# Order of quarter products, their additions and the first down pages in a transformer block

## The chip, the cores and the metric

The kernel runs on one core of a Trainium2 chip. The metric is the device time of one execution in microseconds. Engines: PE (TensorE, matmuls), DVE (VectorE), ACT (ScalarE), POOL (GpSimd), SP (SyncE, which here only issues DMAs). Each engine works through its own queue of instructions in order and waits on semaphores for the others.

## The reference, cut

One layer on x of 1024 x 1024 (float32), D_FF = 2816:

```
h = rmsnorm(x, norm1_g); proj = h @ w_in
mixed = concat(forgetting_attention(q, k, v, log_f), multiscale_pool(u))
x = x + mixed @ w_out
h2 = rmsnorm(x, norm2_g)
gate = h2 @ w_gate
up = h2 @ w_up
x = x + (silu(gate) * up) @ w_down
return rmsnorm(x, final_g)
```

The change lies in the products with w_gate, w_up and w_down.

## The kernel before, in words

**Numbers.** A float32 matrix is kept as two fp32r halves: `split` (L119 to L121) lets ACT copy the hi half (L120) and DVE subtract it for the lo half (L121). A product of two such matrices is three matmuls (`mm3`, L161 to L163: hi·hi, hi·lo, lo·hi), added up in a PSUM bank.

**Gate/up stage.** The 2816 columns are 22 tiles of 128, taken as 11 pairs j = 0 to 10. Each pair is computed by a scheme of seven block products P1 to P7 (in the manner of Strassen and Winograd) instead of eight. Their left operands are blocks of the normed activations (b11, b21, t1 to t4, b22), made once; their right operands are sums of the pair's weight blocks (`gu_sums`, L1070 to L1073, on POOL), split into "pages". From pair 1 on the order is P1, P2, P6, P7, P5, P3a, P4, P3b. A page is made two products ahead (`next_page`).

**The quartered third product.** For j ≥ 1, P3 is itself computed by seven quarter products Q1 to Q7 of 256 columns (`fine_product`), in three banks: A takes Q1, Q6, Q5, Q3 in turn, B takes Q7, Q4, and C takes Q2. After each quarter DVE adds the bank's state into a copy in SBUF (the "sU4" snapshot, L1249), and the next quarter in that bank waits for this add. The page of P3 is made in two parts (P3a, P3b) after subtractions on DVE (`fine_page`, L1214). The quarter sums of the block b22 are made once, in pair 1 (`fine_steps`, up to three steps after each product: DVE's L1189 and L1196 in before, then a split); Q4's operand overwrites b22h/b22l.

**What leaves a pair.** `corner` makes the features h11, h22 and h21: DVE adds bank and snapshot into q (L1154; one buffer), ACT applies silu (L1155), DVE forms h (L1156), POOL multiplies (L1157) and so frees q. h12 is made of the snapshot after P3b (L1272, L1273). `feature_sum` makes f1 to f4 of these (L1162). `spill` stores the features to DRAM (L1254), as a DMA on ACT's queue, behind which ACT waits for the feature; the last pair's last ones go on POOL's queue.

**Down stage.** 28 steps (4 groups of pairs, 7 products each): w_down is loaded (`down_raw`, L1356), summed on POOL for the first group (`down_sum`, L1364), the features are loaded back (`down_load`, L1375), both are split into pages (`down_page`, tiles d0_0 to d0_3 and so on: features hi and lo, weights hi and lo), multiplied into banks d, and added to the residual x2f (L1512). The final norm follows.

**What sets the order.** A scheduler with a simulated timeline orders each engine's instructions; `tc.issue_after(ins)` pins what is issued inside it behind an instruction of the same engine. `mark["mm"]` is the last matmul written so far, `mark["hi"]` ACT's last hi half.

Of the kernel before, what the change touches and what calls it, by code (L numbers as in the profile page):

```python
# [15 lines left out]
P = 128  # L16
# [29 lines left out]
def tile_kernel(  # L46
# [1099 lines left out]
    def corner(j, name, key, src, to):  # L1146

        h = feature(j, name, to)
        q = wk_tile("q", 1, f"q{name}_{j}")
        if key is None:  # L1150
            nc.scalar.activation(out=q, in_=banks[src, 0], func=AF.Silu)
            nc.vector.tensor_tensor(out=h, in0=banks[src, 1], in1=q, op=ALU.mult)
        else:
            nc.vector.tensor_tensor(out=q, in0=banks[src, 0], in1=snaps[j, key, 0], op=ALU.add)  # L1154
            nc.scalar.activation(out=q, in_=q, func=AF.Silu)  # L1155
            nc.vector.tensor_tensor(out=h, in0=banks[src, 1], in1=snaps[j, key, 1], op=ALU.add)  # L1156
            nc.gpsimd.tensor_tensor(out=h, in0=h, in1=q, op=ALU.mult)  # L1157

    def feature_sum(j, name, key, a, b, op):
        t = feature(j, name, key)  # L1160
        eng = nc.gpsimd if j + 1 < NG else nc.vector
        eng.tensor_tensor(out=t, in0=feats[a], in1=feats[b], op=op)  # L1162

    QTR = (slice(0, 256), slice(256, 512))
    fine = {}
# [67 lines left out]
    def fine_product(j, k, q, acc):  # L1233

        at = FINE_BANK[q]
        if q in ("Q1", "Q7", "Q2"):
            fine_banks[at] = bank(f"fine{at}_{j}{k}", *((BANKS["c2", 0], 1) if at == "C" else ("m", 2)))
        ps = fine_banks[at][:, QTR[0]]
        wh, wl = fine[j, k, q]
        bh, bl = fine[BLOCK[k], q]  # L1240
        for c in range(2):
            ws = slice(c * P, (c + 1) * P)
            mm3(
                ps, wh[:, ws], wl[:, ws], bh[:, c, :], bl[:, c, :],
                q in ("Q1", "Q7", "Q2") and c == 0, q in ("Q3", "Q4", "Q2") and c == 1, True,
            )
        n, h = FINE_TO[q]
        out = acc[n][:, QTR[h]]
        nc.vector.tensor_tensor(out=out, in0=ps, in1=out, op=ALU.add)  # L1249

    def spill(q=nc.scalar):
        while spills:
# [6 lines left out]
    def after(j, k):  # L1259
        if k in ("P1", "P6", "P5"):  # L1260
            for n in range(2):
                snap(j, dict(P1="sP1", P6="sU2", P5="sU4")[k], n)
        if k == ("P2" if j else "P5"):
            with tc.issue_after(at.ins) if j == 0 else ExitStack():
                corner(j, "h11", "sP1", "c2", "P1")
        if k == h22_from(j):
            corner(j, "h22", "sU4", "c3", "P4")
        if k == "P3":
            corner(j, "h12", None, "c1", None)
        if k == "P3b":  # L1270
            acc = [snaps[j, "sU4", n] for n in range(2)]
            nc.scalar.activation(out=acc[0], in_=acc[0], func=AF.Silu)  # L1272
            nc.vector.tensor_tensor(out=acc[1], in0=acc[1], in1=acc[0], op=ALU.mult)  # L1273
            feats["h12"] = acc[1]
        if k in ("P3", "P3b"):
            feature_sum(j, "f1", "P5", "h12", "h22", ALU.add)
            feature_sum(j, "f2", "P6", "f1", "h11", ALU.subtract)
            feature_sum(j, "f3", "P7", "h11", "h12", ALU.subtract)
        if k == "P4":
            corner(j, "h21", "sU2", "c3", "P2")  # L1280
        if k == ("P3b" if j else "P4"):
            feature_sum(j, "f4", "P3", "h21", "f2", ALU.subtract)
# [19 lines left out]
    for i, (j, k) in enumerate(todo):  # L1302
        if i + 2 < len(todo):
            next_page(*todo[i + 2])
        if i:
            spill()
        if i == 1:
            product(j, k, 0, (0, 1))
            with tc.issue_after(mark["turn", ORDER[-1]].ins):
                product(j, k, 0, (2, 3))  # L1310
                product(j, k, 1)
        elif i and (k in ("P3a", "P3b") or k == "P4" and j):
            acc = [snaps[j, "sU4", n] for n in range(2)]
            pieces = dict(
                P3a=("Q1", "Q2", "Q7", (0, (0, 1)), "Q4"), P4=((0, (2, 3)), "Q6", (1, (0, 1)), "Q5", (1, (2, 3))),
                P3b=("Q3",),
            )
            for piece in pieces[k]:
                if isinstance(piece, str):
                    fine_product(j, "P3", piece, acc)  # L1320
                else:
                    product(j, "P4", *piece)
# [14 lines left out]
    GROUPS = ((0, 1), (2, 3, 4), (5, 6, 7), (8, 9, 10))  # L1337
    ORDER2 = ("P1", "P2", "P6", "P7", "P5", "P4", "P3")
    BANK1 = ("z2", "tp0", "z0", "z1")
    BANK3 = (("m", 2), ("m", 2), ("tp1", 1), ("po", 1))  # L1340
    PAGES = (("t3h", "t3l", "t1h", "t1l"), ("b22h", "b22l", "t4h", "t4l"))
    SUMS = dict(P5="b21h", P6="b21l", P7="t2h", P4="t2l")
    steps2 = [(b, k) for b in range(len(GROUPS)) for k in ORDER2]
    moving, stationary, raw2 = {}, {}, {}
    late = {}

    def down_raw(b, par):

        g = GROUPS[b]
        if b == 0:  # L1350
            t = blk_tile(("b11h", "b11l")[par], [P, len(g), D], F32, f"r_wd{par}_{b}")
        else:
            t = late["p"].tile([P, len(g), D], F32, tag=f"wd{par}", bufs=1, name=f"r_wd{par}_{b}")
        for i, j in enumerate(g):
            f = 2 * j + par
            nc.sync.dma_start(out=t[:, i, :], in_=w_down[0, f * P : (f + 1) * P, :])  # L1356
        moving[b, ("P1", "P2")[par]] = t[:, :, 0:512]
        moving[b, ("b12", "P3")[par]] = t[:, :, 512:D]

    def down_sum(b, k):  # L1360
        a0, a1 = dict(P5=("b12", "P1"), P6=("P3", "P5"), P7=("P3", "b12"), P4=("P2", "P6"))[k]
        t = blk_tile(SUMS[k], [P, len(GROUPS[b]), 512], F32, f"sum{k}_{b}")
        eng = nc.gpsimd if b == 0 or (b, k) == (1, "P5") else nc.vector
        eng.tensor_tensor(out=t, in0=moving[b, a0], in1=moving[b, a1], op=ALU.subtract)  # L1364
# [108 lines left out]
    for i, (b, k) in enumerate(steps2):  # L1473
# [16 lines left out]
        for c in range(NT // 2):  # L1490
# [66 lines left out]
```

## Time and profile before

| | us |
|---|---|
| three runs | 1057.71, 1059.73, 1060.38 |
| median | 1059.73 |
| profiled execution | 1058.13 |
| its span in the trace | 1056.4 |
| around the span | 1.73 |

The stages by the trace, with PE's busy time and granted clock:

| stretch, us | PE busy | clock |
|---|---|---|
| 380 to 480 (pairs 0 and 1) | 96.77 of 100 | 1.00 |
| 480 to 800 (pairs 2 to 9) | 314.23 of 320 | 1.00 |
| 800 to 850 (last pair, first down products) | 41.08 of 50 | 0.90 |
| 850 to 1056 (down stage, final norm) | 199.57 of 206 | 0.99 |

A timeline row reads: start, duration, engine, line, operation, out<-in, shape, and in brackets the idle time of the engine before it with what ended it. A duration includes fill and drain; matmuls overlap, so their price is the step from one start to the next. In the trace's names `gu_P`, `fineA_8P`, `d` are PSUM tiles or pages; numbers are partly left out.

### The profile page before, as it was taken

To read this page: it belongs to the slowest core of one execution; us is meant where nothing else is said; L and a number is where in the kernel's file an instruction comes from. 1 tells how busy PE (TensorE), PEld (TensorE's weight loads), DVE (VectorE), ACT (ScalarE), POOL (GpSimd) and SP (SyncE) were. 2 spreads that over 40 slices of the span, in tenths; PEclk is the share of its full clock that TensorE was granted. 3 is DMA by queue.
4 is the path that set the end of the run, shared out by engine and by line. 5 is a ranking of instruction groups with operands and counts; after the bars stand their busy time and mean duration, and the time that the engine had idled before them with its cause. 6 is when DMAs were issued, how large, how long until landed. Compare 5 with 4: busy or idle time off the path is not lost. (4 is left out here: it accounts for less than half of the span.)

```text
span 1056.4 us, 14666 instructions
## 1 busy us (share of the span) xinstructions
PE 1028.6 (97%) x5284; PEld 875.0 (83%) x5284; DVE 696.8 (66%) x1132; ACT 462.8 (44%) x747; POOL 390.8 (37%) x314
## 2 busy tenths in 40 slices
PE   9999999999999999999999999999999699999997
PEld 8988888998888888787888888888888588888886
DVE  7464566776886499775535545544546699888886
ACT  7334355665664276343324323333333234333346
POOL 4450121223443150736555654654757110000035
PEclk9999999999999999999999999999999899999999
DMA  7224334233932241432323322323226745353424
GB/s 246 52 65 141 84 86 112 62 101 86 313 115 66 85 140 60 132 118 100 100 90 110 100 100 102 108 90 124 95 90 229 267 162 179 105 184 130 150 90 160
DMA packets 108313, 130.25 MB, mean 123 GB/s; under 512 B 7368, under 2 KB 70352, under 8 KB 108240
## 3 DMA queue, kind: packets, MB, share of 16 engines
q1 hardware_dynamic: 96544, 108.18, 32.4%
q10 hardware_dynamic: 11216, 19.95, 4.9%
q0 software_dynamic: 480, 1.18, 0.4%
q8 instruction: 42, 0.69, 0.3%
q14 instruction: 31, 0.25, 0.1%
HBM read 86.29 MB, written 33.03 MB: 113 GB/s over the span
## 5 line engine op out<-in xcount | busy, mean ns | idle before, releaser
L162 PE MATMUL d<-d,d 128*128 128x512 f32 (+1 forms) x308 | 120.6, 392 | 0.0
L163 PE MATMUL d<-d,d 128*128 128x512 f32 (+1 forms) x308 | 118.4, 388 | 0.0
L629 POOL TENSOR_SCALAR p<-p,rr 128x128 f32<-128x128 f32 (+3 forms) x64 | 48.8, 767 | 177.0 <-DVE rr L628 152.0
L161 PE MATMUL d<-d,d 128*128 128x512 f32 x308 | 109.6, 392 | 4.5 <-ACT d L120 4.5
L120 ACT ACTIVATE d<-r_f 128x1536 fp32r<-128x1536 f32 (+1 forms) x28 | 38.8, 1384 | 117.8 <-PE d L162 115.0
L161 PEld LDWEIGHTS d<-d,d 128*128 128x128 f32 x308 | 58.5, 190 | 16.9 <-ACT d L120 4.8
L120 ACT ACTIVATE gu_P_h<-r 128x1024 fp32r<-128x1024 f32 x32 | 33.6, 1055 | 88.0 <-POOL h L1157 44.5
L1070 POOL TENSOR_TENSOR s<-r 128x1024 f32<-128x1024 f32 x10 | 24.0, 2403 | 124.9 <-DMA r<-in_w_up_dram 124.9
L162 PEld LDWEIGHTS d<-d,d 128*128 128x128 f32 x308 | 58.6, 190 | 12.7 <-DVE d L121 0.6
L163 PEld LDWEIGHTS d<-d,d 128*128 128x128 f32 x308 | 57.8, 188 | 11.9
L121 DVE TENSOR_TENSOR gu_P_l<-r,gu_P_h 128x1024 fp32r<-128x1024 f32 x32 | 54.4, 1702 | 14.5 <-ACT gu_P_h L120 14.5
L626 ACT ACTIVATE p<-p,mn 128x128 f32<-128x128 f32 (+3 forms) x64 | 49.4, 773 | 31.7 <-DVE mn L620 28.7
L1157 POOL TENSOR_TENSOR h<-h,qh 128x512 f32<-128x512 f32 x33 | 53.8, 1631 | 24.3 <-issue 13.9
L1418 POOL TENSOR_SCALAR sse<-sse 128x1 f32<-128x1 f32 x7 | 3.5, 496 | 158.0 <-ACT junk L1414 158.0
L121 DVE TENSOR_TENSOR gu_P_l<-s,gu_P_h 128x1024 fp32r<-128x1024 f32 (+1 forms) x38 | 45.4, 1223 | 21.8 <-ACT gu_P_h L120 21.7
L648 DVE TENSOR_TENSOR tl<-tp,th 128x512 fp32r<-128x512 f32 (+1 forms) x80 | 49.5, 633 | 9.8 <-ACT th L647 8.7
L1154 DVE TENSOR_TENSOR qh<-gu_P,sn_sU 128x512 f32<-128x512 f32 x22 | 15.2, 690 | 54.4 <-POOL h L1157 42.6
L121 DVE TENSOR_TENSOR d<-r_f,d 128x1536 fp32r<-128x1536 f32 (+1 forms) x28 | 46.0, 1641 | 7.4 <-ACT d L120 7.4
L163 PE MATMUL qk<-hTh,l_qk 128*128 128x512 f32 x128 | 50.7, 396 | 0.0
L161 PE MATMUL qk<-hTh,h_qk 128*128 128x512 f32 x128 | 50.6, 395 | 0.0
L162 PE MATMUL qk<-hTl,h_qk 128*128 128x512 f32 x128 | 50.4, 394 | 0.0
L1512 DVE TENSOR_TENSOR x2f_s<-d,x2f_s 128x512 f32<-128x512 f32 x64 | 42.7, 685 | 11.5 <-PE d L163 11.4
(806 smaller groups left out, 3226.3 us busy)
## 6 DMA issues: line engine op xcount, KB each, us to landing
r_f<-hsdP SPq DMA_DIRECT2D x77, 256.0 KB
r_wd<-in_w_down_dram SPq DMA_DIRECT2D x22, 512.0 KB
r<-in_w_gate_dram SPq DMA_DIRECT2D x21, 512.0 KB
r<-in_w_up_dram SPq DMA_DIRECT2D x21, 512.0 KB
hsdP<-f ACTq DMA_DIRECT2D x40, 256.0 KB
hsdP<-h ACTq DMA_DIRECT2D x33, 256.0 KB
s<-hi SPq DMA_DIRECT2D x64, 128.0 KB
x<-in_x_dram SPq DMA_DIRECT2D x8, 512.0 KB
```

What stands on the lines that cost most here:

```text
L120: mark["hi"] = nc.scalar.activation(out=hi, in_=src, func=AF.Copy)
L121: return eng.tensor_tensor(out=lo, in0=src, in1=f32(hi), op=ALU.subtract)
L161: nc.tensor.matmul(ps, lh, rh, start=start, stop=False, **kw)
L162: nc.tensor.matmul(ps, lh, rl, start=False, stop=False, **kw)
L163: mark["mm"] = nc.tensor.matmul(ps, ll, rh, start=False, stop=stop, **kw)
L626: nc.scalar.activation(out=pr[:, :n], in_=pr[:, :n], func=AF.Exp, scale=-1.0, bias=mn, accum_out=rs)
L629: nc.gpsimd.tensor_scalar(out=pr[:, :n], in0=pr[:, :n], scalar1=rr, scalar2=1.0, op0=ALU.mult, op1=ALU.mult)
L648: nc.vector.tensor_tensor(out=tl[:, :w], in0=tp[:, :w], in1=f32(th[:, :w]), op=ALU.subtract)
L1070: g(out=s1, in0=a21, in1=a22, op=ALU.add)
L1154: nc.vector.tensor_tensor(out=q, in0=banks[src, 0], in1=snaps[j, key, 0], op=ALU.add)
L1157: nc.gpsimd.tensor_tensor(out=h, in0=h, in1=q, op=ALU.mult)
L1512: added = nc.vector.tensor_tensor(out=row, in0=ps, in1=row, op=ALU.add)
```

## The change

It edits the gate/up loop and the start of the down stage:

1. `feature_sum` is always on POOL; before, the last pair's four sums were on DVE.
2. The quarter adds of one pair are pinned on DVE in written order, each behind the one before.
3. The corner h21 of pairs 1 to 10 is made after P3b, pinned behind the last add, instead of after P4.
4. The quarters and pieces of P4 are written in another order, and each is pinned on PE behind the piece before it. `(n, cs)` is a piece of P4: half n, chunks cs.
5. `fine_steps` begin after pair 1's P2 instead of its P1.
6. In the last pair the down stage's first loads, sums and page are issued between the products: w_down after P1, the sums P5 and P6 (now on DVE) after P6, the loads of the first two feature pages after P7 (into tiles of tags s2 and s1), the first page after P3a. Page 1 is pinned behind the last add; the last pair's final features are pinned on ACT's side behind page 1; the sums P7 and P4 stay on POOL. The first down product is pinned behind the closing matmul of Q3.

The diff, cut (the definitions of the down stage that only move up are left out):

```diff
     def feature_sum(j, name, key, a, b, op):
         t = feature(j, name, key)
-        eng = nc.gpsimd if j + 1 < NG else nc.vector
-        eng.tensor_tensor(out=t, in0=feats[a], in1=feats[b], op=op)
+        nc.gpsimd.tensor_tensor(out=t, in0=feats[a], in1=feats[b], op=op)
...
-        nc.vector.tensor_tensor(out=out, in0=ps, in1=out, op=ALU.add)
+        with tc.issue_after(mark["add"].ins) if q != "Q1" else ExitStack():
+            mark["add"] = nc.vector.tensor_tensor(out=out, in0=ps, in1=out, op=ALU.add)
...
+        if k == ("P3b" if j else "P4"):
+            with tc.issue_after(mark["add"].ins) if j else ExitStack():
+                corner(j, "h21", "sU2", "c3", "P2")
...
-        if k == "P4":
-            corner(j, "h21", "sU2", "c3", "P2")
...
-        eng = nc.gpsimd if b == 0 or (b, k) == (1, "P5") else nc.vector
+        eng = nc.gpsimd if (b, k) in ((0, "P7"), (0, "P4"), (1, "P5")) else nc.vector
...
+        if i < 2:
+            r = xw_tile(f"s{2 - i}", f"r_f{i}", (P, n, 512))
...
-                P3a=("Q1", "Q2", "Q7", (0, (0, 1)), "Q4"), P4=((0, (2, 3)), "Q6", (1, (0, 1)), "Q5", (1, (2, 3))),
+                P3a=("Q1", "Q2", "Q7", (0, (0, 1)), (0, (2, 3)), "Q6", "Q4"), P4=((1, (0, 1)), "Q5", (1, (2, 3))),
                 P3b=("Q3",),
...
+                with tc.issue_after(mark["mm"].ins):
...
-        after(j, k)
-        if j == 1 and k == "P1":
+        if (j, k) == (NG - 1, "P3b"):
+            last_features = lambda j=j, k=k: after(j, k)
+        else:
+            after(j, k)
+        if j == NG - 1:
+            if k == "P1":
+                for par in range(2):
+                    down_raw(0, par)
+            if k == "P6":
+                for key in ("P5", "P6"):
+                    down_sum(0, key)
+            if k == "P7":
+                for par in range(2):
+                    down_load(par)
+            if k == "P3a":
+                down_page(0)
+        if j == 1 and k == "P2":
             finer += fine_steps("b22")
...
-    for par in range(2):
-        down_raw(0, par)
-        down_load(par)
-    down_page(0)
-    down_page(1)
-    for k in ("P5", "P6", "P7", "P4"):
+    closing = mark["mm"]
+    with tc.issue_after(mark["add"].ins):
+        down_page(1)
+    with tc.issue_after(mark["hi"].ins):
+        last_features()
+    for k in ("P7", "P4"):
         down_sum(0, k)
...
+                with tc.issue_after(closing.ins) if i == 0 else ExitStack():
+                    mm3(
```

What stands on the engines, first DVE in pair 8 (one of pairs 2 to 9, which are alike), from Q1's add on. `sn8_sU40` and `sU41` are the two halves of the snapshot that the adds go into, `fineA/B/C` the banks, `gu9_P1_l` the lo half of the next pair's first page. Before:

```order
L1249 TENSOR_TENSOR sn8_sU40_7499<-fineA_8P3_7525,sn8_sU40_7499 128x256
L121 TENSOR_TENSOR gu8_P3b_l_7513<-s4_8_7220,gu8_P3b_h_7512 128x768
L1156 TENSOR_TENSOR h22_8_7503<-gu8_P71_7455,sn8_sU41_7501 128x512
L1249 TENSOR_TENSOR sn8_sU40_7499<-fineC_8P3_7533,sn8_sU40_7499 128x256
L1249 TENSOR_TENSOR sn8_sU41_7501<-fineB_8P3_7541,sn8_sU41_7501 128x256
L1154 TENSOR_TENSOR qh21_8_7599<-gu8_P70_7442,sn8_sU20_7430 128x512
L1249 TENSOR_TENSOR sn8_sU41_7501<-fineB_8P3_7541,sn8_sU41_7501 128x256
L1249 TENSOR_TENSOR sn8_sU41_7501<-fineA_8P3_7525,sn8_sU41_7501 128x256
L1156 TENSOR_TENSOR h21_8_7598<-gu8_P71_7455,sn8_sU21_7432 128x512
```

Now, from h22 on:

```order
L1156 TENSOR_TENSOR h22_8_7503<-gu8_P71_7455,sn8_sU41_7501 128x512
L1249 TENSOR_TENSOR sn8_sU40_7499<-fineC_8P3_7533,sn8_sU40_7499 128x256
L1249 TENSOR_TENSOR sn8_sU41_7501<-fineB_8P3_7541,sn8_sU41_7501 128x256
L1249 TENSOR_TENSOR sn8_sU41_7501<-fineA_8P3_7525,sn8_sU41_7501 128x256
L1249 TENSOR_TENSOR sn8_sU41_7501<-fineB_8P3_7541,sn8_sU41_7501 128x256
L121 TENSOR_TENSOR gu9_P1_l_7576<-r0_9_7439,gu9_P1_h_7575 128x1024
L1249 TENSOR_TENSOR sn8_sU41_7501<-fineA_8P3_7525,sn8_sU41_7501 128x256
L121 TENSOR_TENSOR gu9_P2_l_7599<-r0_9_7439,gu9_P2_h_7598 128x1024
L1213 TENSOR_TENSOR s4_9_7519<-s4_9_7519 128x256
L1249 TENSOR_TENSOR sn8_sU40_7499<-fineA_8P3_7525,sn8_sU40_7499 128x256
L1154 TENSOR_TENSOR qh21_8_7612<-gu8_P70_7442,sn8_sU20_7430 128x512
L1156 TENSOR_TENSOR h21_8_7611<-gu8_P71_7455,sn8_sU21_7432 128x512
```

qh21 stood between Q7's add and those of Q4 and Q6; now the adds are in the order Q1, Q2, Q7, Q6, Q4, Q5, Q3, and qh21 stands behind the last.

The second place is DVE in the last pair, from P3a's lo half on (`s4_10` is the quarter subtraction for P3b's page, `gu10_P4_l` P4's lo half, `d0_1` and `d0_3` the lo halves of the first down page, `d1_3` one of the second). Before:

```order
L1214 TENSOR_TENSOR s4_10_7818<-s4_10_7818 128x256 x3
L121 TENSOR_TENSOR gu10_P4_l_8064<-r1_10_7771,gu10_P4_h_8063 128x1024
L1154 TENSOR_TENSOR qh22_10_8096<-gu10_P70_8037,sn10_sU40_8091 128x512
L1249 TENSOR_TENSOR sn10_sU40_8091<-fineA_10P3_8109,sn10_sU40_8091 128x256
L121 TENSOR_TENSOR gu10_P3b_l_8105<-s4_10_7818,gu10_P3b_h_8104 128x768
L1156 TENSOR_TENSOR h22_10_8095<-gu10_P71_8050,sn10_sU41_8093 128x512
L1249 TENSOR_TENSOR sn10_sU40_8091<-fineC_10P3_8117,sn10_sU40_8091 128x256
L121 TENSOR_TENSOR d0_3_8220<-r_wd0_0_8205,d0_2_8219 128x1024
L1249 TENSOR_TENSOR sn10_sU41_8093<-fineB_10P3_8125,sn10_sU41_8093 128x256
L1154 TENSOR_TENSOR qh21_10_8179<-gu10_P70_8037,sn10_sU20_8028 128x512
L1156 TENSOR_TENSOR h21_10_8178<-gu10_P71_8050,sn10_sU21_8030 128x512
L1249 TENSOR_TENSOR sn10_sU41_8093<-fineB_10P3_8125,sn10_sU41_8093 128x256
```

Now:

```order
L1213 TENSOR_TENSOR s4_10_7818<-s4_10_7818 128x256 x3
L121 TENSOR_TENSOR gu10_P4_l_8080<-r1_10_7771,gu10_P4_h_8079 128x1024
L121 TENSOR_TENSOR d0_1_8176<-r_f0_8073,d0_0_8175 128x1024
L1154 TENSOR_TENSOR qh22_10_8112<-gu10_P70_8047,sn10_sU40_8107 128x512
L1249 TENSOR_TENSOR sn10_sU40_8107<-fineA_10P3_8125,sn10_sU40_8107 128x256
L121 TENSOR_TENSOR gu10_P3b_l_8121<-s4_10_7818,gu10_P3b_h_8120 128x768
L1156 TENSOR_TENSOR h22_10_8111<-gu10_P71_8060,sn10_sU41_8109 128x512
L1249 TENSOR_TENSOR sn10_sU40_8107<-fineC_10P3_8133,sn10_sU40_8107 128x256
L121 TENSOR_TENSOR d0_3_8178<-r_wd0_0_7963,d0_2_8177 128x1024
L1249 TENSOR_TENSOR sn10_sU41_8109<-fineB_10P3_8141,sn10_sU41_8109 128x256
L1249 TENSOR_TENSOR sn10_sU41_8109<-fineA_10P3_8125,sn10_sU41_8109 128x256
L1249 TENSOR_TENSOR sn10_sU41_8109<-fineB_10P3_8141,sn10_sU41_8109 128x256
```

d0_1, which came after the last add, now stands ahead of qh22; d0_3 keeps its place between Q2's and Q7's add; d1_3 moves behind h21. The sums P5 and P6 stand just ahead of these rows, around P5's lo half.

The third place is DVE in pair 1. Before, the operand of Q4 (`b22l`) was split long ahead of the quarter adds:

```order
L121 TENSOR_TENSOR fine2l_b22_5249<-fine_b2211_5295,fine2h_b22_5248 128x512
L1214 TENSOR_TENSOR s4_1_5095<-s4_1_5095 128x256
L121 TENSOR_TENSOR b22l_4444<-fine_b2210_5370,b22h_4443 128x2x256
L1214 TENSOR_TENSOR s4_1_5095<-s4_1_5095 128x256 x2
L121 TENSOR_TENSOR gu1_P4_l_5376<-r1_1_5089,gu1_P4_h_5375 128x1024
```

Now:

```order
L1156 TENSOR_TENSOR h22_1_5405<-gu1_P71_5352,sn1_sU41_5403 128x512
L1188 TENSOR_TENSOR fine_b2210_5411<-b22h_4443,b22l_4444 128x512
L1249 TENSOR_TENSOR sn1_sU40_5401<-fineC_1P3_5440,sn1_sU40_5401 128x256
L1249 TENSOR_TENSOR sn1_sU41_5403<-fineB_1P3_5448,sn1_sU41_5403 128x256
L1195 TENSOR_TENSOR fine_b2210_5411<-fine_b2210_5411,fine_b2211_5328 128x512
L121 TENSOR_TENSOR b22l_4444<-fine_b2210_5411,b22h_4443 128x2x256
L1249 TENSOR_TENSOR sn1_sU41_5403<-fineA_1P3_5432,sn1_sU41_5403 128x256
L1249 TENSOR_TENSOR sn1_sU41_5403<-fineB_1P3_5448,sn1_sU41_5403 128x256
```

It is made between the adds of Q7 and Q6.

More of the change, by code (lines that the diff above doesn't have):

```diff
@@ new lines, in tile_kernel, with down_raw @@
+    SUMS = dict(P5="b21h", P6="b21l", P7="t2h", P4="t2l")
+    steps2 = [(b, k) for b in range(len(GROUPS)) for k in ORDER2]
+    moving, stationary, raw2 = {}, {}, {}
+    late = {}
+    def down_raw(b, par):
+        g = GROUPS[b]
+        if b == 0:
+            t = blk_tile(("b11h", "b11l")[par], [P, len(g), D], F32, f"r_wd{par}_{b}")
+        else:
+            t = late["p"].tile([P, len(g), D], F32, tag=f"wd{par}", bufs=1, name=f"r_wd{par}_{b}")
+        for i, j in enumerate(g):
+            f = 2 * j + par
+            nc.sync.dma_start(out=t[:, i, :], in_=w_down[0, f * P : (f + 1) * P, :])
+        moving[b, ("P1", "P2")[par]] = t[:, :, 0:512]
+        moving[b, ("b12", "P3")[par]] = t[:, :, 512:D]
@@ L1284, in tile_kernel, with down_page @@
+    def down_page(i):
+        b, k = steps2[i]
+        n = len(GROUPS[b])
+        fh, fl, wh, wl = (blk_tile(t, [P, n, 512], R, f"d{i}_{m}") for m, t in enumerate(PAGES[i % 2]))
+        split(wh, wl, moving[b, k])
+        split(fh, fl, raw2.pop(i))
+        stationary[i] = fh, fl, wh, wl
     LATER = ("P1", "P2", "P6", "P7", "P5", "P3a", "P4", "P3b")
@@ L1345, in tile_kernel @@
[L1345 to L1358, printed above, removed]
```

66 lines of the change are left out of this document (28 added, 38 removed).

## Prediction

> **What bounds the kernel now.** I read the page's table of engines first, then the windows, then PE's waits, and then the timeline around each wait.
>
> ```profile
> PE 1028.6 (97%) x5284; PEld 875.0 (83%) x5284; DVE 696.8 (66%) x1132; ACT 462.8 (44%) x747; POOL 390.8 (37%) x314
> ```
> PE (TensorE) is busy for 1028.6 of 1056.4 us, and nothing in the change alters the number of matmuls. So a change can only bring what PE now idles, or what it loses to a lower clock. The windows show where that is (columns: window, length, busy us and instructions of PE, PEld, DVE, ACT, POOL, then granted clock, DMA share, GB/s).
>
> ```profile
> 440.00:480.00 40.00, 38.85 (x185) 31.91 (x185) 30.69 (x39) 15.64 (x22) 23.35 (x13) 1.00 0.32 105
> 480.00:800.00 320.00, 314.23 (x1534) 263.96 (x1535) 158.71 (x216) 111.73 (x150) 175.20 (x91) 1.00 0.32 105
> 800.00:850.00 50.00, 41.08 (x187) 34.05 (x186) 34.16 (x35) 14.29 (x18) 22.36 (x15) 0.90 0.74 270
> 831.00:838.00 7.00, 2.15 (x7) 1.85 (x8) 4.50 (x8) 1.83 (x3) 1.92 (x4) 0.51 0.73 264
> ```
> Pairs 2 to 9 of the gate/up stage (480 to 800) idle 320 − 314.23 = 5.77 us. The end of the last pair and the start of the down stage (800 to 850) idle 8.92 us, at a clock of 0.51 for a part of it. PE's waits, by releaser (us in total, times, longest):
>
> ```profile
> PE d L161 <- ACT d L120: 4.5, 1, 4.5
> PE fineA_10P L161 <- DVE sn_sU L1249: 3.4, 2, 2.9
> PE gu_P L163 <- DVE gu_P_l L121: 2.8, 2, 2.3
> PE fineA_2P L161 <- DVE sn_sU L1249: 1.1, 1, 1.1
> PE gu_P L161 <- DVE qh L1154: 1.0, 1, 1.0
> PE fineA_4P L161 <- DVE sn_sU L1249: 0.5, 1, 0.5
> ```
> One wait of 0.5 to 1.1 us in each of pairs 2 to 9, all at the fifth quarter product Q5, is the 5.77. Pair 8 shows its cause:
>
> ```profile
> 741.46 2.41 POOL L1070 TENSOR_TENSOR s<-r 128x1024 f32<-128x1024 f32 x1 [12.23 <-DMA r<-in_w_up_dram]
> 743.83 2.39 POOL L1072 TENSOR_TENSOR s<-r,r 128x1024 f32<-128x1024 f32 x1
> 746.18 1.29 POOL L1157 TENSOR_TENSOR h<-h,qh 128x512 f32<-128x512 f32 x1
> ```
> ```profile
> 747.51 0.69 DVE L1154 TENSOR_TENSOR qh<-gu_P,sn_sU 128x512 f32<-128x512 f32 x1 [4.92 <-POOL h L1157]
> 748.57 0.42 DVE L1249 TENSOR_TENSOR sn_sU<-fineA_8P,sn_sU 128x256 f32<-128x256 f32 x1
> ```
> ```profile
> 744.62 0.28 PE L163 MATMUL fineA_8P<-fine2h_b,gu_P3b_l 128*128 128x256 f32 x1
> 748.00 0.40 PE L163 MATMUL gu_P<-t4h,gu_P_l 128*128 128x512 f32 x1
> 749.05 0.39 PE L161 MATMUL fineA_8P<-fine_b,gu_P3b_h 128*128 128x256 f32 x1 [0.66 <-DVE sn_sU L1249]
> ```
> DVE's qh21 (L1154) waits 4.92 us for its one buffer, which POOL's h22 (L1157) frees at 747.47 behind two sums of 2.4 us. Behind qh21 in DVE's queue stand the adds of Q4 and Q6, so Q6's add, whose matmuls ended near 744.74, runs to 748.99, and Q5 starts at 749.05.
>
> **The change part by part.** The prices of a matmul come first.
>
> ```profile
> 843.07 0.39 PE L163 MATMUL d<-d,d 128*128 128x512 f32 x1
> 850.33 1.07 PE L161 MATMUL d<-d,d 128*128 128x512 f32 x4
> ```
> ```profile
> 816.45 0.28 PE L161 MATMUL fineA_10P<-b22h,gu_P3a_h 128*128 128x256 f32 x1
> 818.49 0.28 PE L163 MATMUL fineB_10P<-fine3h_b,gu_P3a_l 128*128 128x256 f32 x1
> ```
> 32 matmuls of 512 columns lie between 843.07 and 850.33: .227 us each. 17 of 256 columns lie between 816.45 and 818.49: .12 each, .72 for a quarter product. In pair 8 the step from 748.00 to 749.05 is 1.05, so the wait shown as .66 costs 1.05 − .23 = .82: each wait of an otherwise full PE costs .16 more than it shows.
>
> *Pairs 2 to 9 (corner h21 moved behind the last add, adds in written order, pieces reordered).* Q6 now stands right behind Q7 in the chain of adds and qh21 is no longer ahead. Between Q6's end and Q5 lie now Q4 (.72) and six matmuls (1.36), 2.08 us, where Q6's add needs .42 and its wake-up. Its cover is 1.6 us larger than the need, so the wait goes. What is late next is the pair's own Q5 add behind the next pair's P1 lo half; its reader Q3 stands after 20 more matmuls, so nothing. h21 later: its bank is wanted again only by the next pair's P7, three products on (24 matmuls, 5.4 us each); no cost. On ACT the next page's hi half moves ahead of h22's store, which only brings it earlier. Gain 5.77 + 8 × .16 = **7.1** (6 to 7.1 if a tenth stays).
>
> *Pair 1 (fine_steps one product later).*
>
> ```profile
> 476.69 0.38 PE L161 MATMUL fineA_1P<-fine_b,gu_P3b_h 128*128 128x256 f32 x1 [0.28 <-DVE sn_sU L1249]
> 479.93 0.50 PE L163 MATMUL gu_P<-b11h,gu_P_l 128*128 128x512 f32 x1 [0.45 <-DVE gu_P_l L121]
> ```
> ```profile
> 463.42 0.69 DVE L121 TENSOR_TENSOR b22l<-fine_b,b22h 128x512 fp32r<-128x512 f32 x1
> ```
> ```profile
> 470.42 1.29 POOL L1157 TENSOR_TENSOR h<-h,qh 128x512 f32<-128x512 f32 x1 [13.93 <-issue]
> ```
> ```profile
> 821.07 0.58 ACT L1135 ACTIVATE sn_sU<-gu_P 128x512 f32<-128x512 f32 x1
> ```
> The two waits go: .28 + .45 + 2 × .16 = 1.06. But the operand that Q4 reads, b22h/b22l, was ready at 464.11 and is now made among pair 1's own adds. In before Q5 was due at 476.24; pair 8's pattern put at that place makes Q4 due 3.5 us earlier, at 472.8. Its inputs: the L1195 subtraction of two SBUF tiles, held until POOL's h22 ends at 471.71 (+.69 = 472.4), then ACT's hi (as many columns as the .58 row) and the .69 lo half: 473.7 if POOL's next sum lets DVE in, 474.5 or more if not. Wait 1.7 (1.0 to 5, the upper end if two 2.4 us sums go first). Net **−.6**.
>
> *The last pair and the seam.*
>
> ```profile
> 819.81 0.50 PE L161 MATMUL gu_P<-t4h,gu_P_h 128*128 128x512 f32 x1 [1.05 <-DVE qh L1154]
> 829.89 0.39 PE L161 MATMUL fineA_10P<-fine_b,gu_P3b_h 128*128 128x256 f32 x1 [2.89 <-DVE sn_sU L1249]
> 831.39 0.58 PE L161 MATMUL fineA_10P<-b22h,gu_P3b_h 128*128 128x256 f32 x1 [0.52 <-DVE sn_sU L1249]
> 837.50 0.80 PE L161 MATMUL d<-d,d 128*128 128x512 f32 x1 [4.46 <-ACT d L120]
> ```
> From Q1's start (816.45) to the third down product (850.33) are 33.88 us. The work in it is 42 quarter matmuls (5.0) and 24 + 48 matmuls (16.4): 21.4. The loss is thus 12.4: the waits 1.05, 2.89, .52 and 4.46, and the halved clock. What replaces it depends on DVE, and there on POOL:
>
> ```profile
> 732.05 1.22 DVE L1214 TENSOR_TENSOR s<-s 128x256 f32<-128x256 f32 x3
> 809.33 6.49 DVE L1214 TENSOR_TENSOR s<-s 128x256 f32<-128x256 f32 x3
> 823.00 2.21 DVE L121 TENSOR_TENSOR d<-r_wd,d 128x1024 fp32r<-128x1024 f32 x1
> 837.48 1.23 DVE L121 TENSOR_TENSOR d<-r_f,d 128x1024 fp32r<-128x1024 f32 x1
> ```
> ```profile
> 804.57 2.39 POOL L1364 TENSOR_TENSOR sumP<-r_wd 128x1024 f32<-128x1024 f32 x1 [0.49 <-DMA r_wd<-in_w_down_dram]
> 810.41 2.59 POOL L1364 TENSOR_TENSOR sumP<-r_wd,sumP 128x1024 f32<-128x1024 f32 x1
> 822.83 1.29 POOL L1157 TENSOR_TENSOR h<-h,qh 128x512 f32<-128x512 f32 x1 [4.76 <-DVE h L1156]
> 760.53 1.30 POOL L1162 TENSOR_TENSOR f<-sn_sU,h 128x512 f32<-128x512 f32 x1 [5.14 <-DMA r<-in_w_up_dram]
> ```
> The same three subtractions (L1214) took 1.22 us alone and 6.49 while POOL added the down sums: DVE is held while POOL reads. (The Trainium skill's page "SBUF — State Buffer", section "Who interferes with whom", says that a DVE instruction with two SBUF inputs and a GpSimd one that reads SBUF exclude each other for a whole instruction. The trace agrees, 6.49 against 1.22, and this speaks against f1 to f4 moved to POOL.) Now DVE's chain: sumP5 starts at 804.57, when its load is in; sumP6 ends near 808.2 (its load is in somewhere between 804.57 and 810.41, when POOL's row reads it in before; I take 807, and one sum 1.2). Then P3a's lo half, L1213, P4's lo half and the newly placed d0_1, 1.2 each: 4.9, and two of POOL's sums, P7 and P4, lock 2 × 2.59 of it: 818.3, qh22 to 819.0. P4's first matmul is due at 818.61: wait **.4** (0 to 3.4). Q6 and then Q4 follow; Q4 is due at 819.0 + 2.73 + .72 = 822.46. It waits for Q7's add, ahead of which DVE now has d0_3, behind POOL's h22 (about 822.1 to 823.4), 1.23 long: 824.6, the add to 825.0. Wait **2.5** (1.5 if d0_3 gets in before POOL, up to 2.6). After it Q4, six matmuls, Q5, six, Q3 run through to 829.9. The pages of the first down product are ready by 824.6, so the 4.46 wait is gone, and with no long gap the clock stays up. What is late next is the down stage's third page, whose lo halves meet POOL's f1 to f4 (1.3 us each): **.4** (0 to 2.6, two of them). The second page is split behind Q3's add, h21 and one POOL multiply: at the latest 836.4, wanted at 837.2. On SP the feature loads into s2 and s1 hold up nothing, since this is the last pair. The POOL stores and the later w_down loads behind them on SP are wanted some 20 us later; no cost. Gain 12.3 − 3.3 = **9.0**.
>
> Sum: 7.1 − .6 + 9.0 = 15.5, so the profiled run of 1058.13 would become 1042.6. It lies 1.6 below the median of the three runs, 1059.73; with half of that added: **1043.4**.
>
> **The rivals.**
>
> *C, the clock halves after the new wait* (chance .2). The clock of .51 began near 831 in before, when waits of 1.05 and 2.89 lay behind and the 4.46 still ahead; after the 2.3 wait of pair 1 (window 440 to 480) it stayed at 1.00. The new 2.5 lies between. Half speed for the 8 to 10 us that before shows doubles a part of it: +1.8 to +5, 1046 to 1048. (The Trainium skill's page "TensorE: Matmul & The Clock Gate", section "HAM oscillation — how this bites in real kernels", allows gaps up to about 3.4 us; by it there would be no halving here, and the sum stays 1043.4. The trace halved it after 2.89, so the measurement decides for C as possible.)
>
> *B, the waits in the pairs stay* (.08). If the adds are late for another reason than qh21, as POOL's hold on DVE, the change does not do there what it says: 1043.4 + 7.1 = 1050.5. Against it: adds read PSUM and ran in .42 beside POOL.
>
> *D, the other side: written order against late adds* (.03). If Q6's add still ended at 748.99, Q5, now due at 744.74 + .72 + 1.36 = 746.82, would wait 2.2 instead of .82, with six matmuls behind it that went ahead before: +1.4 in each of 8 pairs, +11 in place of −7.1, about 1061.5. It decides from the point at which Q6's add ends over 2.1 us after Q6. Against it: nothing with a wait is left ahead of that add.
>
> **How the numbers follow.** Main case .66, C .2, B .08, D .03, and .03 for more gain. The main case's own bounds: without pair 1's 1.7 and the two .4, and with 1.5 at Q4, 3.5 better, 1039.8 to 1039.9; with Q4's operand in pair 1 late by 5, or qh22 by 3.4, 3.0 to 3.3 worse, 1046.7. With C and part of B the range is 1039.8 to 1049.5. What a measurement of this kernel can tell from no change is about .3%, 3.2 us. Only D, and B together with a failed seam, reach 1056.5 or more: faster .94, same .03, slower .03.
>
> **What would show it.** Right: no Q5 wait in pairs 2 to 9 and PE busy over 319 of their 320 us; one wait of 1 to 2.5 at pair 1's Q4, for b22l; in the last pair a wait of 1.5 to 2.6 at Q4 for Q7's add with d0_3 ahead of it on DVE; the first d matmul right after Q3; clock 1.00 throughout. Wrong: any Q5 or Q3 wait that recurs in each pair, a clock near .5 after Q4, or a first d matmul that waits over 2 us.

## The result, and the profile after

The changed kernel takes 1044.93 us (median of five runs, 1042.36 to 1045.78), the kernel before 1059.73 (five runs, 1057.71 to 1060.38). The ratio is 0.9857, with a 95% interval of 0.9838 to 0.9877. The forecast was 1043.4, with a range of 1039.8 to 1049.5. The profiled execution is that of 1044.93, with a span of 1043.2.

The page and the windows of the changed kernel, with the columns of the prediction's windows:

```profile
PE 1026.5 (98%) x5284; PEld 876.5 (84%) x5284; DVE 715.2 (69%) x1130; ACT 465.9 (45%) x747; POOL 410.6 (39%) x317
```
```profile
440.00:480.00 40.00, 38.22 (x178) 31.84 (x178) 28.57 (x36) 15.08 (x21) 22.13 (x12) 0.97 0.31 105
480.00:800.00 320.00, 320.00 (x1571) 271.25 (x1569) 181.08 (x221) 118.02 (x154) 198.39 (x96) 1.00 0.34 113
800.00:850.00 50.00, 47.86 (x222) 39.74 (x221) 42.86 (x47) 18.05 (x21) 20.74 (x15) 0.97 0.69 245
```

From 480 to 800 PE idles nowhere. From 440 to 480 it idles more than before, 1.78 in place of 1.15, and the granted clock is 0.97. From 800 to 850 it idles 2.14 in place of 8.92. Its waits:

```profile
PE gu_P L163 <- DVE gu_P_l L121: 2.3, 1, 2.3
PE fineB_10P L161 <- DVE sn_sU L1249: 2.1, 1, 2.1
PE fineB_1P L162 <- DVE b22l L121: 1.7, 1, 1.7
...
PE d L162 <- DVE d L121: 1.1, 2, 0.6
```

The first was there before (pair 1's P2 page). The second is Q4 in the last pair, the third Q4 in pair 1. The last line stands for two waits of .64 and .45 that were not forecast; they lie at 853 and 864, in the down stage.

Where the time went is best read between places at which the same work has been done: the start of Q1 in pairs 1, 2 and 10 (the first `fineA` matmul of the pair), the start of the third down product, and the end.

| stretch | before | after | difference |
|---|---|---|---|
| start to Q1 of pair 1 | 467.15 | 467.00 | −.15 |
| to Q1 of pair 2 | 39.06 | 40.05 | +.99 |
| to Q1 of pair 10 (eight pairs) | 310.24 | 302.24 | −8.00 |
| to the third down product (the seam) | 33.88 | 25.66 | −8.22 |
| to the end of the span | 206.07 | 208.25 | +2.18 |

The sum is −13.2, the difference of the spans. Pair 8 in the changed kernel, first DVE and then PE:

```profile
736.78 0.41 DVE L1249 TENSOR_TENSOR sn_sU<-fineB_8P,sn_sU 128x256 f32<-128x256 f32 x1
739.54 0.42 DVE L1249 TENSOR_TENSOR sn_sU<-fineA_8P,sn_sU 128x256 f32<-128x256 f32 x1 [2.35 <-PE fineA_8P L163]
740.26 0.42 DVE L1249 TENSOR_TENSOR sn_sU<-fineB_8P,sn_sU 128x256 f32<-128x256 f32 x1 [0.30 <-PE fineB_8P L163]
...
749.35 0.68 DVE L1154 TENSOR_TENSOR qh<-gu_P,sn_sU 128x512 f32<-128x512 f32 x1
```
```profile
739.22 0.28 PE L163 MATMUL fineA_8P<-fine2h_b,gu_P3b_l 128*128 128x256 f32 x1
...
741.45 0.28 PE L161 MATMUL fineA_8P<-fine_b,gu_P3b_h 128*128 128x256 f32 x1
```

Q6's last matmul starts at 739.22, its add follows at 739.54 and now waits for PE alone, and ends at 739.96; Q5 starts at 741.45, 1.5 us later, with no wait. qh21 stands at 749.35, where nobody waits for it. In pair 1, POOL's h22, the L1195 subtraction and the lo half of Q4's operand on DVE, and the wait on PE:

```profile
469.94 1.62 POOL L1157 TENSOR_TENSOR h<-h,qh 128x512 f32<-128x512 f32 x1 [15.54 <-issue]
```
```profile
470.98 1.12 DVE L1195 TENSOR_TENSOR fine_b<-fine_b,fine_b 128x512 f32<-128x512 f32 x1
472.80 2.08 DVE L121 TENSOR_TENSOR b22l<-fine_b,b22h 128x512 fp32r<-128x512 f32 x1 [0.70 <-ACT b22h L120]
```
```profile
474.94 0.39 PE L162 MATMUL fineB_1P<-b22l,gu_P3a_h 128*128 128x256 f32 x1 [1.73 <-DVE b22l L121]
```
In the seam, DVE, POOL and PE:

```profile
814.84 2.25 DVE L121 TENSOR_TENSOR d<-r_wd,d 128x1024 fp32r<-128x1024 f32 x1
817.00 0.41 DVE L1249 TENSOR_TENSOR sn_sU<-fineB_10P,sn_sU 128x256 f32<-128x256 f32 x1
```
```profile
814.72 1.28 POOL L1157 TENSOR_TENSOR h<-h,qh 128x512 f32<-128x512 f32 x1 [7.08 <-issue]
```
```profile
817.47 0.38 PE L161 MATMUL fineB_10P<-b22h,gu_P3a_h 128*128 128x256 f32 x1 [2.09 <-DVE sn_sU L1249]
...
818.42 0.63 PE L161 MATMUL gu_P<-t4h,gu_P_h 128*128 128x512 f32 x1
818.85 0.63 PE L162 MATMUL gu_P<-t4l,gu_P_h 128*128 128x512 f32 x1
...
824.04 0.39 PE L161 MATMUL d<-d,d 128*128 128x512 f32 x1
```

d0_3 takes 2.25 instead of 1.2, and POOL's h22, 1.28 long, began .12 us ahead of it; Q7's add comes behind, and Q4 waits for that. Then the matmuls step by .43 instead of .23 from 818.42 on: the clock is halved for about 3 us (0.50 granted between 818.1 and 821.4). The first down product starts at 824.04, right after Q3 (823.92).

### The profile page after: what moved, and what is told of

It reads as the page before. It is cut to its first block, busy times and chain, and to the rows that moved or that the text cites. A ratio compares the mean times of both kernels' runs of the same rounds, so it can differ in the third digit from the quotient of the medians.

```text
span 1043.2 us, 14702 instructions
## 1 busy us (share of the span) xinstructions
PE 1026.5 (98%) x5284; PEld 876.5 (84%) x5284; DVE 715.2 (69%) x1130; ACT 465.9 (45%) x747; POOL 410.6 (39%) x317
## 4 chain that ended last, share of the span: by engine, by line
PE 47%; DVE 5%; DMA 2%; issue 1%; ACT 0%; POOL 0%; POOLq 0%; ACTq 0%; DVEq 0%; SPq 0%
PE gu_P L162 9%; PE gu_P L161 9%; PE gu_P L163 9%; PE d L162 5%; PE d L163 5%; PE d L161 5%; DVE d L121 2%; DVE x2f_s L1532 1%; DMA x2f_s<-x2d 1%; DVE x2f_r L1532 1%; DMA r_wd<-in_w_down_dram 0%; DVE gu_P3a_l L121 0%; DMA gfb<-in_final_g_dram 0%; DVE s L1213 0%; DVE b22l L121 0%
## 5 line engine op out<-in xcount | busy, mean ns | idle before, releaser
L1157 POOL TENSOR_TENSOR h<-h,qh 128x512 f32<-128x512 f32 x33 | 61.9, 1875 | 54.3 <-ACT qh L1155 29.9
L121 DVE TENSOR_TENSOR gu_P_l<-s,gu_P_h 128x1024 fp32r<-128x1024 f32 (+1 forms) x38 | 51.6, 1365 | 18.9 <-ACT gu_P_h L120 18.8
L647 ACT ACTIVATE th<-tp 128x512 fp32r<-128x512 f32 (+1 forms) x80 | 42.5, 550 | 16.7 <-PE tp L643 13.9
```

The source lines that it names most:

```text
L121: return eng.tensor_tensor(out=lo, in0=src, in1=f32(hi), op=ALU.subtract)
L647: nc.scalar.activation(out=th[:, :w], in_=tp[:, :w], func=AF.Copy)
```

## The experiments

Times are medians; each kernel was timed beside the kernel before on the same chip, and the ratio is to that, with its 95% interval. Where stretches are given, they are those of the table above. The kernel before had medians of 1059.73, 1058.38, 1058.0 and 1059.32 on the occasions of the study, so up to 1.7 us between medians of two different occasions say little; the stretches of the profiles say more.

**One part alone: h21 moved.** In the kernel before (the line that sets `mark["add"]` is left out):

```diff
+        if k == ("P3b" if j else "P4"):
+            with tc.issue_after(mark["add"].ins) if j else ExitStack():
+                corner(j, "h21", "sU2", "c3", "P2")
...
-        if k == "P4":
-            corner(j, "h21", "sU2", "c3", "P2")
```

> The kernel before with one part of the change: corner h21 behind the last quarter add; the order of matmuls stays that of before. Theory (qh21 ahead of the adds of Q4 and Q6 is the whole cause of the waits in pairs 2 to 9): the Q5 waits vanish there, 5.77 of idle and about 1.3 of restart, 7.1 in all: 1059.7 - 7.1 = 1052.6, with PE busy over 319 of 320 us between pairs 2 and 9, and the seam to the down stage as long as before. Rival (the order of the quarter products carries the gain, by putting Q4 and six matmuls between Q6 and Q5): the adds are still late, half or more of the waits stay, 1056 or more.

Measured: 1053.8 us, ratio 0.9955 (0.9938 to 0.9972). Pairs 2 to 9:

```profile
480.00:800.00 320.00, 319.88 (x1563) 268.32 (x1563) 175.04 (x219) 115.34 (x154) 178.70 (x94) 1.00 0.34 112
```

No wait is left there, and the eight pairs take 303.96, so h21 alone brings 6.28 of the 8.00, and the rival falls. (The medians, 1058.38 and 1053.8, show only 4.6; the runs of this kernel lie 6 us apart.) The rest shows in pair 8:

```profile
742.20 0.42 DVE L1249 TENSOR_TENSOR sn_sU<-fineB_8P,sn_sU 128x256 f32<-128x256 f32 x1 [4.67 <-PE fineB_8P L163]
742.66 0.42 DVE L1249 TENSOR_TENSOR sn_sU<-fineA_8P,sn_sU 128x256 f32<-128x256 f32 x1
```
```profile
743.17 0.36 PE L161 MATMUL fineA_8P<-fine_b,gu_P3b_h 128*128 128x256 f32 x1
743.37 0.28 PE L162 MATMUL fineA_8P<-fine_b,gu_P3b_h 128*128 128x256 f32 x1
```

Q4's add stands ahead of Q6's, although Q6 was done earlier on PE. So Q6's add ends at 743.08, and Q5 starts at 743.17, too late by so little that the page shows no wait, but with a step of .20 to the next matmul instead of .12.

**One part alone: written order.** The kernel before with the chained adds and the pieces in the new order, pinned; corner h21 is left after P4.

```diff
+        with tc.issue_after(mark["add"].ins) if q != "Q1" else ExitStack():
+            mark["add"] = nc.vector.tensor_tensor(out=out, in0=ps, in1=out, op=ALU.add)
...
-                P3a=("Q1", "Q2", "Q7", (0, (0, 1)), "Q4"), P4=((0, (2, 3)), "Q6", (1, (0, 1)), "Q5", (1, (2, 3))),
+                P3a=("Q1", "Q2", "Q7", (0, (0, 1)), (0, (2, 3)), "Q6", "Q4"), P4=((1, (0, 1)), "Q5", (1, (2, 3))),
...
+                with tc.issue_after(mark["mm"].ins):
...
```

> The kernel before with two parts of the change: the quarter adds chained and the quarters and pieces of P4 in the written order; corner h21 stays after P4, so that the scheduler may place it. DVE's queue then has qh21 behind Q4's add and the next P1 lo half, ahead of Q5's add. Theory (what counts is that qh21 is not ahead of Q6's add, however that comes about): no Q5 waits either, 1052.6. Rival D of the prediction (the written order with late adds): +1.4 in each of 8 pairs, about 1071.

Measured: 1047.33 us, ratio 0.9894 (0.9879 to 0.9909), lower than either theory had it. The eight pairs take 302.24, the whole gain. In pair 8 the scheduler, not a pin, now has qh21 behind Q6's add, and that add waits for PE alone:

```profile
736.13 0.42 DVE L1250 TENSOR_TENSOR sn_sU<-fineA_8P,sn_sU 128x256 f32<-128x256 f32 x1 [2.35 <-PE fineA_8P L163]
739.63 0.68 DVE L1154 TENSOR_TENSOR qh<-gu_P,sn_sU 128x512 f32<-128x512 f32 x1
```

So the two parts are not added up: either one takes qh21 from ahead of Q6's add, and the order does the remaining 1.7 as well. Beside that, pair 1 takes 37.77 instead of 39.06: its two waits of .28 and .45 are gone too, and without a new one, since the sums of b22 are as early as before. The seam is 33.02, nearly as before. Of the 11.3 us between the two profiles another 1.3 lie ahead of pair 1 (465.86 instead of 467.15); what brought these is not shown.

**All but the seam.** The kernel before with everything but the down stage's part and the last features on POOL (the hunks on `feature_sum`, `down_sum`, `down_load`, the last pair and the first down product left out).

> All of the change but the down stage's part and the last pair's sums on POOL: the seam is as before. Theory: the pairs give 7.1, pair 1 costs .6 to 1 (a wait of 1.7 for b22l for two of .28 and .45), so 1053.2 to 1054; the seam is then worth 1053.6 - 1044.9 = 8.7, near the predicted 9.0. Rival (the seam's gain comes from the order of the last pair's quarters, not from moving the down stage's page and sums): 1049 or less.

Measured: 1052.87 us, ratio 0.9947 (0.9934 to 0.996). The eight pairs take 302.24 and the seam 34.96, so what the down stage's part is worth there is 34.96 − 25.66 = 9.3 between the two profiles. The gains over the kernel before differ by as much: 5.5 here, 14.8 for the changed kernel. The rival falls. Pair 1 takes 41.64, 2.6 more than before, with the wait of 1.72 for b22l and a halved clock behind it. Against order_only it differs by h21 (nothing left to gain) and by the sums of b22 begun later, and is 5.5 us slower by medians; 3.9 us of the profiles' difference lie in pair 1.

**The sums of b22 early again.** The changed kernel with one word changed back:

```diff
-        if j == 1 and k == "P2":
+        if j == 1 and k == "P1":
             finer += fine_steps("b22")
```

> The changed kernel with the quarter sums of b22 begun after pair 1's P1, as before. Theory: the wait of 1.73 at pair 1's Q4 (2.0 by starts) goes and nothing takes its place: 1044.9 - 2.0 = 1042.9. Rival (the sums were spread because they delay the pages of P6 and P7 on DVE): a wait in pair 1 grows by as much, 1044.9 or more.

Measured: 1039.76 us, ratio 0.9821 (0.9807 to 0.9835): 5.2 us less than the changed kernel by medians, and a gain over the kernel before of 18.6 instead of 14.8, so 3.8 to 5.2 in place of the 2.0 expected. Its waits:

```profile
PE gu_P L163 <- DVE gu_P_l L121: 2.5, 1, 2.5
PE fineB_10P L161 <- DVE sn_sU L1249: 2.1, 1, 2.1
...
PE d L162 <- DVE d L121: 1.2, 2, 0.7
```

The wait for b22l is gone and no other has grown by more than .24; pair 1 takes 37.77 in place of 40.05, which is 2.3. The rest of the 4.8 between the profiles is mostly the clock, which here stays whole behind both long waits: the last pair's Q4 waits 2.09 as before, the matmuls behind it step by .12 and .23, and the seam takes 23.81 instead of 25.66.

**d0_3 behind Q4's add.**

```diff
-        split(wh, wl, moving[b, k])
+        with tc.issue_after(mark["add"].ins) if i == 0 else ExitStack():
+            split(wh, wl, moving[b, k])
```

> The changed kernel with the weights' half of the first down page (d0_2 on ACT, d0_3 on DVE) pinned behind Q4's add instead of ahead of Q7's. Theory (d0_3 and POOL's h22 ahead of Q7's add are the wait of 2.09 at the last pair's Q4, and the halved clock behind it, 1.5 in the profile, comes of that wait): Q4 waits at most .3, 1044.9 - 2.0 - 1.5 = 1041.4, or 1042.9 where the clock had not halved. Rival (Q7's add is late anyway, behind h22 and P3b's lo half): Q4 still waits over 1, 1044.

Measured: 1042.2 us, ratio 0.9845 (0.9831 to 0.9858). The pin holds DVE's d0_3 only; ACT's d0_2 stays early. Q4 no longer waits, d0_3 takes 1.22, and the seam takes 21.71 instead of 25.66, within .3 of the 21.4 that its matmuls need. So d0_3 ahead of Q7's add was the wait, and without the wait the clock did not halve there. In this profile 2.3 us are lost again in pair 1, where the wait for b22l was longer and the clock halved (columns as in every timeline):

```profile
475.49 0.43 PE L162 MATMUL fineB_1P<-b22l,gu_P3a_h 128*128 128x256 f32 x1 [2.44 <-DVE b22l L121]
...
476.56 0.63 PE L161 MATMUL gu_P<-t4h,gu_P_h 128*128 128x512 f32 x1
476.99 0.63 PE L162 MATMUL gu_P<-t4l,gu_P_h 128*128 128x512 f32 x1
```

**The last features back on DVE.** `eng = nc.gpsimd if j + 1 < NG else nc.vector`, as before, in the changed kernel.

> The changed kernel with the last pair's sums f1 to f4 back on DVE. Theory (on POOL they lock DVE's lo halves of the third page, 2.11 and 2.31 instead of 1.22, which the cover there hides): DVE gains 2 us from the lock and pays 4 x .69 = 2.8, so no change, 1044.4 to 1045.5. Rival by the skill-independent reading of the rows (the lock puts DVE behind and so makes the later waits of .64 and .45 in the down stage): these go, 1043.5.

Measured: 1045.63 us, ratio 0.9886 (0.9872 to 0.9899). The seam is the same to .05 (25.71). The down stage still has waits, of .25 and .81, so the rival falls as well: f1 to f4 on POOL are not their cause. By its ratio this kernel gains .003 less than the changed one, but the two intervals meet (.9872 and .9877): the engine of these four sums decides nothing that these runs can tell.

**fine_early and d03_late together.**

> fine_early and d03_late together. Theory (the two waits are independent): fine_early's 1039.8 less 2.0 for the Q4 wait: 1037.8, and lower by up to 1.5 if the clock was halved there in some of fine_early's runs. Rival (what is late next takes it back): 1039 or more.

Measured: 1036.55 us, ratio 0.98 (0.9786 to 0.9813). Pair 1 takes 37.83, the seam 21.74. Each edit takes off its own wait and leaves the other's stretch alone, as the theory had it.

**The same, and the second group's sum P5 on DVE.** `down_sum` with `(1, "P5")` taken out of the list for POOL.

> Both, and the down stage's sum P5 of the second group on DVE instead of POOL. Theory (POOL's 4.39 there holds a DVE lo half for 4.52 instead of 1.22, and this is the source of the two waits of .64 and .45, 1.4 by starts): 1.4 less than both. Rival (DVE has no room: the sum's own 1.7 on DVE delays the same lo halves): as both or slower.

Measured: 1037.38 us, ratio 0.9803 (0.979 to 0.9816): no gain. In `both` the two waits of the down stage were not there to begin with; here one of .51 is, and the runs of the two kernels overlap, as the rival said. In the changed kernel's first profile POOL's sum fell on a lo half of DVE, in `both` on adds that read PSUM:

```profile
848.67 4.52 DVE L121 TENSOR_TENSOR d<-sumP,d 128x1024 fp32r<-128x1024 f32 x1
```
```profile
842.78 2.58 DVE L1533 TENSOR_TENSOR x2f_s<-d,x2f_s 128x512 f32<-128x512 f32 x4
```
```profile
847.72 4.39 POOL L1312 TENSOR_TENSOR sumP<-r_wd 128x1536 f32<-128x1536 f32 x1 [9.09 <-DVE x2f_s L1532]
```
```profile
842.16 4.08 POOL L1312 TENSOR_TENSOR sumP<-r_wd 128x1536 f32<-128x1536 f32 x1 [10.55 <-DMA r_wd<-in_w_down_dram]
```

The first row of each pair is the changed kernel, the second `both`. A lo half of 1.2 became 4.52; four adds that read PSUM took 2.58 instead of 2.47. The other profiles agree: where POOL's sum met that lo half (the changed kernel, fine_early and d03_late with 4.52, feats_dve with 3.78), two waits of PE follow; where it met the adds (after_again, `both`, both_sums1, late_adds), none does. Which of the two it meets comes and goes with the run.

**Pair 1's weight sums off POOL.** `both`, with s2 and s3 of pair 1 issued on DVE behind P2's lo half (the part in `gu_sums` that hands them over is left out):

```diff
...
+        if (j, k) == (1, "P2"):
+            with tc.issue_after(mark["page"].ins):
+                later.pop()(nc.vector.tensor_tensor)
```

> Both, and pair 1's weight sums s2 and s3 on DVE behind P2's lo half instead of on POOL ahead of it. Theory (the wait of 2.0 to 2.5 at pair 1's P2, which before has too, is DVE held by POOL's two sums; a clock that halves there comes of it): the wait goes, 1036.6 - 2.2 = 1034.4. Rival (the sums' 2.4 us on DVE delay P6's lo half or the pair 0 corner by as much): 1036 or more.

Measured: 1034.99 us (1032.96 to 1035.69), ratio 0.9767 (0.9752 to 0.9782). The wait of 2 us at pair 1's P2 is gone, and with it the last long one. Over `both` this brings 1.6 by medians and 2.9 by the gains over the kernel before (2.2 expected), so the rival falls. The list of PE's waits still holds these and three of .2 to .3:

```profile
PE warm L254 <- DVE junk L252: 1.2, 1, 1.2
PE gu_P L161 <- DVE qh L1163: 0.3, 1, 0.3
```

This is the version to keep: its interval lies below that of `both`, and it is 24.7 us below the kernel before (.0233 of 1059.32) and 9.9 by medians below the changed one.

**Late adds again.** The changed kernel with DVE's first step of h21 (`qh21`) for pairs 2 to 9 pinned between the adds of Q7 and Q6, as the kernel before had it (the definition of `corner_q`, which issues qh21, is left out).

```diff
...
+                if piece == "Q6" and 2 <= j < NG - 1:
+                    corner_q(j)
```

> The changed kernel with qh21 of pairs 2 to 9 pinned between Q7's and Q6's add, where the kernel before had it, so that the adds are late again while the written order stays. This prices rival D of the prediction. Theory: Q6's add ends when POOL's h22 has freed q, so Q5 waits 2.2 in each of 8 pairs where before waited .82: 1044.9 + 8 x 2.2 = 1062.5, slower than before. Rival (the adds are not late for qh21's sake, or POOL's queue is earlier now): under 1052.

Measured: 1051.28 us, ratio 0.9927 (0.9914 to 0.9941): far from the theory's 1062.5. It is under the rival's 1052, but not for its reasons. The eight pairs take 309.83, 7.6 more than without the edit, and lose their time at another place (pair 8, DVE and then PE):

```profile
748.52 1.79 DVE L121 TENSOR_TENSOR gu_P_l<-r,gu_P_h 128x1024 fp32r<-128x1024 f32 x1 [4.09 <-ACT gu_P_h L120]
750.24 0.68 DVE L1151 TENSOR_TENSOR qh<-gu_P,sn_sU 128x512 f32<-128x512 f32 x1
750.84 0.41 DVE L1258 TENSOR_TENSOR sn_sU<-fineA_8P,sn_sU 128x256 f32<-128x256 f32 x1
```
```profile
749.38 0.39 PE L162 MATMUL gu_P<-b11l,gu_P_h 128*128 128x512 f32 x1
750.37 0.50 PE L163 MATMUL gu_P<-b11h,gu_P_l 128*128 128x512 f32 x1 [0.60 <-DVE gu_P_l L121]
```

The adds are late again (Q6's at 750.84, 4.3 us after its last matmul at 746.46). But Q5 does not wait for them, since the scheduler put the next pair's P1 ahead of Q5 on PE, and its lo half ahead of qh21 on DVE: a pin says "behind", not "directly behind". P1 in turn waits .5 to 1.1 for its lo half in each of the eight pairs. So this run does not price late adds with the next matmuls left in place; what it shows is what the scheduler makes of them.

**The changed kernel once more,** for a second profile.

> The changed kernel unchanged, for a second profile. Question: whether a halved clock behind a wait of about 2 us belongs to the kernel or to chance. If to the kernel: halved from 439 to 442.7 and behind the last pair's Q4 as in the first profile, 1044.9. If to chance: one or none of the two, 1041.3 to 1043.5.

Measured: 1044.44 us. The time is the first profile's, but made up in another way: the clock stays whole at 439, the wait for b22l is 2.42 with a halved clock behind it (pair 1 takes 42.30 instead of 40.05), Q4's wait is 2.09 with a halved clock as before, and the down stage has neither of its two waits (206.52 to the end instead of 208.25). So the halved clock at 439 and the waits at 853 and 864 come and go with the run. Neither branch of the expectation holds as it stands: at two places the same kernel did both, and that the sum came out equal is luck.

## Why the prediction was right, step by step

Between the two profiles 13.2 us went, where 15.5 were forecast: .9 more in pairs 2 to 9, .4 less in pair 1, .8 less in the seam, and 2.2 lost behind it; .15 came ahead of pair 1. The mechanisms below are those of the forecast, with the two exceptions that are named (the clock and the down stage). That the time came so near is in part luck, since the misses have both signs and the second profile has other ones. Three slips are in the working: 33.88 − 21.4 is 12.5, not 12.4 and 12.3; the price of restarting was added to the waits that go, but not to those that come; and 1043.4 + 1.8 is 1045.2, not the 1046 at which rival C begins.

**Pairs 2 to 9: right in the mechanism, the size a little low.** 7.1 was forecast, 8.00 measured. The term that was mis-sized is the price of restarting: a wait costs more than it shows not by .16 but by .27, because the second step after it is long too. Pair 8 in before, from Q5's first matmul on, which the page gives a wait of .66:

```profile
749.05 0.39 PE L161 MATMUL fineA_8P<-fine_b,gu_P3b_h 128*128 128x256 f32 x1 [0.66 <-DVE sn_sU L1249]
749.27 0.29 PE L162 MATMUL fineA_8P<-fine_b,gu_P3b_h 128*128 128x256 f32 x1
749.39 0.28 PE L163 MATMUL fineA_8P<-fine_b,gu_P3b_l 128*128 128x256 f32 x1
```

The first step is .22, the next .12, as usual. Over the eight waits, 5.77 by the page, the step into the wait and the one behind it are together 7.95 longer than usual, which is the 8.00. That qh21 was the cause is shown by h21_only. What the forecast did not see is that the written order alone is enough. Rival B (the waits stay) falls.

**Pair 1: right in the mechanism, the cost too low.** A wait of 1.7 (1.0 to 5) for b22l was forecast; it is 1.73 and, in the second profile, 2.42. The chain is the one described: L1195 held by POOL's h22, then ACT, then the lo half under POOL's next sum (2.08 instead of .69). The net of −.6 was −1.0 and −3.2. The two old waits gave 1.29 (39.06 − 37.77 of order_only; 1.06 forecast), but the wait of 1.73 cost 2.28 (40.05 − 37.77) where the sum had 1.7; in the second profile the wait was longer and the clock halved behind it, which was not in the sum. fine_early shows that this part of the change is a loss.

**The seam: right in kind, 8.2 instead of 9.0.** The wait of 4.46 is gone, with the halved clock behind it. The wait at Q4 is 2.09 (2.5 forecast, 1.5 to 2.6), for the reason given: d0_3 behind POOL's h22. P4's first matmul is .2 late by its start, too little to be listed (.4 forecast). What the sum did not have is the clock, which halved behind Q4: 1.85, by the 25.66 here and the 23.81 of fine_early, where Q4 waits as long and the clock stays whole.

**Rival C came true in part.** It had a chance of .2 and +1.8 to +5. The clock did halve behind the new wait, in both profiles of the changed kernel, but for 3 us only, so at 1.9 each time (25.66 and 25.73 against 23.81). So one of the prediction's own signs of being wrong, a clock near .5 after Q4, did appear, and its "clock 1.00 throughout" failed; the main case had said that the clock stays up, and its sum has nothing for it. The Trainium skill's page "TensorE: Matmul & The Clock Gate", section "HAM oscillation — how this bites in real kernels", allows gaps of up to about 3.4 us without this. The measurement differs: in the profiles of this study it happened behind waits of 1.72 to 2.46 us.

**Rival D was priced without the scheduler.** It was given +11 if the adds stayed late. In late_adds, the one run with the written order and late adds, the eight pairs lose 7.6, no more than before lost there, because the scheduler fills the gap with the next pair's P1. What D would cost with the matmuls left in place is not shown.

**The down stage: not foreseen.** .4 (0 to 2.6) was allowed for one place behind the seam; 2.18 were lost, most of it in two waits of .64 and .45 further on, behind a lo half on which POOL's sum fell. In the second profile they were absent and .45 was lost. The lock by f1 to f4 that the forecast named is there (lo halves of 2.11 and 2.31 instead of 1.2), but it costs PE only .2: the third down product takes 1.34 from its start to its sixth matmul, and 1.14 in feats_dve, which lacks the lock.

## What to carry to other kernels

In an engine's queue, look for the instruction that waits for a slow other engine and for what stands behind it: moving that one (qh21 behind POOL's multiply) freed eight waits on PE, and either of two edits did it, so their gains must not be added. A step that is spread out "to make room" has a reader with a due time: the quarter sums moved one product later missed theirs. And a DVE step with two SBUF inputs is better not placed ahead of an add that TensorE waits for, next to a POOL instruction: d0_3 ahead of Q7's add cost 4 us of the seam in the profile (half of it by the halved clock; 2.7 between the medians), and placed behind Q4's add it delayed nothing.

## What the runs showed of the hardware

TensorE's clock halved behind waits of about 2 us, and not behind each of them. In the profiles of this study there are 26 waits of PE of 1.72 to 2.51 us at three places (pair 1's P2 page, pair 1's Q4, and Q4 or Q5 in the last pair). Behind 14 of them the matmuls step at half speed (.43 instead of .23), for some 3 to 4 us, which costs 1.5 to 2; in one of the 14 (h21_only, last pair) another wait of .52 lies between. At the first place it was 3 of 12, at the second 5 of 6, at the third 6 of 8, and the same kernel gave both (at 439, waits of 2.27 halved and 2.20 not). What decides it is not shown by these runs. Two such places could make up the 3.4 us by which the runs of the changed kernel lie apart, but only two of its runs have a profile, so that is not shown. Where the clock halves, a gap of 2 us on PE costs nearly twice its length.
